# Delta-rule and retention gates in pairs of chunks, half of their rows as seven block products for eight

## The chip, the cores and the metric

The kernel runs on one core of a Trainium2 chip. The core has five engines that run side by side, each working through its own list of instructions in order: PE (matrix products), DVE (element-wise vector work), ACT (activations and copies), POOL (a small general engine) and SP (which here only issues transfers). Sixteen DMA engines move data between the chip's memory (HBM) and the core's own (SBUF, 128 partitions). Products are summed in PSUM, eight banks of 128x512 float32. The metric is the time of one execution on the device in microseconds.

## What is computed

One layer of a streaming encoder on 256 tokens, width 2048, all in float32. `h = rms_norm(x)`; one wide projection of h feeds two token mixers; their outputs are gated, added and projected; then cross-attention into 256 memory tokens and a squared-ReLU MLP. Around the change:

```python
proj = h @ w_in
(rq, rk, rv, rg, gqkv, ga, gb, gz, gate_a, gate_b) = jnp.split(proj, ...)
yr = retention_chunked(rope(rq), rope(rk) * RET_DK ** -0.5, rv)   # then normalised per head
yr = silu(rg) * yr
yg = gated_delta_chunked(gq, gk, gv, log_a, beta)  # per chunk of 64: triangular solve of (eye + m)
yg = silu(gz) * (yg * rsqrt(mean(yg * yg) + NORM_EPS) * gdn_norm_g)
merged = sigmoid(gate_a) * yr + sigmoid(gate_b) * yg
```

rg, gz, gate_a and gate_b are each 2048 columns wide: h (256x2048) times a 2048x2048 part of w_in.

## The kernel before

**Three products for one.** PE multiplies in a faster form of float32 with fewer bits. Each operand is therefore split into a rounded part (hi, copied by ACT) and what is left (lo, subtracted by DVE), and a product is three: hi hi, hi lo, lo hi. For weights, `fetch` (line 106) loads 1 MB into a buffer `raw` (three in turn) on SP's queue, and per half of it (128x1024) ACT writes `whi` (line 124) and DVE `wlo` (line 125), three buffers of each. h stands split in four tiles h1[0..3], each with four of the sixteen 128-row blocks of the inner dimension.

**Chunks.** `chunk` (line 156) makes 512 columns of a projection for all 256 tokens: four fetches of 1 MB (q = 0..3, a quarter of the inner dimension each), and for each 4 blocks x 2 token tiles x 3 products of 128x512, so 96 in all, summed in two banks (`stream_ps`, tags s0 and s1, two of each). `blocks` (line 226) makes 256 columns in turned form for the parts that need features on partitions.

**The mixer** is a loop over four groups j of heads (line 969), each 512 columns wide, with a fifth turn for what is left:

1. `gdn_stream(j)`: projections of q, k, v for the delta rule in two pairs of heads; short convolution; k and q products of a pair (lines 700, 702, "grams"); scaled and masked into `alt`; small diagonal blocks copied into `cmp_l` (line 728). `kq` holds a pair's k and q.
2. `gdn_blocks(j)`: the diagonal blocks go to HBM and come back turned round (`scr_l`, `lw`, lines 755 to 758), a triangular solve of 62 dependent operations on DVE (lines 766 and 768) fills `tw`, which goes out (`scr_t`, line 770) and comes back as `ct` (line 776).
3. `gate_delta_rule(j - 1)` (j > 0): the chunks gz and gate_b of the group before, their gating, then a transpose (`to_feature`).
4. `retention(j)`: two `blocks` projections into `qk`, one chunk of v into `vh` and `vl`, scores and outputs, normalisation.
5. `gdn_core(j)`: the rest of the delta rule, written as steps that `step()` lets run one at a time between the products of the following chunks.
6. `gate_retention(j)`: the chunks rg and gate_a of this group.

So in turn j, groups 1 to 3, the delta-rule gates of group j - 1 follow the projections of group j, and the solve of group j runs beside them; in the fifth turn the gates of group 3 stand alone.

**What sets the order.** A scheduler orders each engine's list when the program is built, by priorities and by data: fetches and roundings have a high priority, and a tile that is written waits until the last reader of what lay in its buffer is done. Tiles with the same tag and `bufs=1` share one buffer. All small PSUM results come from `bank()` (line 74), tag b, four banks in turn. On an engine, an instruction that waits holds up everything behind it.

In the MLP, the second product already uses seven block products for eight (`with_seven`, line 1202), on sums of tokens made by `token_sums`.

Of the kernel before, what the change touches and what calls it, by code (L numbers as in the profile page):

```python
# [54 lines left out]
def trunk(ctx: ExitStack, tc: tile.TileContext, x_f, mem_f, positions, lead_f, small_f, w_blocks, w_chunks, w_ga,  # L55
# [136 lines left out]
    def cols(w, c):  # L192
        return lambda q: w[c, q]
# [472 lines left out]
    def gdn_stream(grp):  # L666
# [3 lines left out]
        for pr in range(2):  # L670
# [17 lines left out]
                r4 = mx.tile([P, 4, NT, GD], F32, name="r4", tag="r4", bufs=1)  # L688
            grams = []
            ssk, ssq = (mx.tile([P, 2, NT], F32, name=nm, tag=nm, bufs=2) for nm in ("ssk", "ssq"))  # L690
            for b in range(2):
                kh = mx.tile([P, 2, S], F32R, name="kh", tag="kh", bufs=2)
                kl = mx.tile([P, 2, S], F32R, name="kl", tag="kl", bufs=2)
                act.activation(kh, kq[:, b], AF.Copy)
                vec.tensor_sub(kl, kq[:, b], kh.bitcast(F32))
                g0, g1 = bank(), bank()
                g0v = g0.rearrange("p (a n) -> p a n", a=2)
                g1v = g1[:, 0:256].rearrange("p (a n) -> p a n", a=2)
                for n, (l, r) in enumerate(((kh, kh), (kh, kl), (kl, kh))):
                    pe.matmul(g0v, l[:, 0, 0:P], r, start=n == 0, stop=n == 2)  # L700
                for n, (l, r) in enumerate(((kh, kh), (kh, kl), (kl, kh))):
                    pe.matmul(g1v, l[:, 0, P:S], r[:, :, P:S], start=n == 0, stop=n == 2)
# [165 lines left out]
    def retention(j, yr):  # L868
# [36 lines left out]
        for t in range(NT):  # L905
            ops = bank()
            for e in range(2):
                es = slice(e * 256, (e + 1) * 256)
                for m in range(t + 1):
                    ns = slice((t + m) * P, (t + m + 1) * P)  # L910
                    three(ops[:, es], [a[:, ns] for a in sts[e]], [a[:, m, es] for a in v], m == 0, m == t)
            mv = mx.tile([P, 2, 2], F32, name="mv", tag="mv", bufs=2)
            for e in range(2):
                bs = mx.tile([P, 6], F32, name="bs", tag="bs", bufs=2)
                vec.bn_stats(bs, ops[:, e * 256:(e + 1) * 256])
                vec.bn_aggr(mv[:, e, :], bs)
            ve = mx.tile([P, 2], F32, name="ve", tag="ve", bufs=2)
            vec.tensor_scalar(ve, mv[:, :, 1], 1e-5, None, op0=ALU.add)
            rg = mx.tile([P, 2], F32, name="rg", tag="rg", bufs=2)
            rsqrt(rg, ve)  # L920
            for e in range(2):
                es = slice(e * 256, (e + 1) * 256)
                vec.tensor_scalar(yr[:, t, es], ops[:, es], mv[:, e, 0:1], rg[:, e:e + 1],
                                  op0=ALU.subtract, op1=ALU.mult)
            vec.tensor_mul(yr[:, t, :], yr[:, t, :], gng)


    def gates():
        def gate_of(ps, f, scale):
            th = mx.tile([P, 512], F32, name="gth", tag="gth", bufs=1)  # L930
            act.activation(th, ps, f, scale=scale)
            return th

        def silu_gate(y):
            def evac(t, ps, c0, c1):
                th = gate_of(ps, AF.Silu, 1.0)
                vec.scalar_tensor_tensor(y[:, t, :], th, 0.5, y[:, t, :], op0=ALU.mult, op1=ALU.mult)
            return evac

        def sig_gate(y, other=None):  # L940
            def evac(t, ps, c0, c1):
                th = gate_of(ps, AF.Tanh, 0.5)
                vec.scalar_tensor_tensor(y[:, t, :], th, 1.0, y[:, t, :], op0=ALU.add, op1=ALU.mult)
                if other is not None:
                    vec.tensor_add(y[:, t, :], y[:, t, :], other[:, t, :])
            return evac

        def of_retention(j, yr):
            chunk(h1, cols(w_chunks, H_RG + j), silu_gate(yr))
            chunk(h1, cols(w_chunks, H_TA + j), sig_gate(yr))  # L950

        def of_delta_rule(j, yr, yg, quad, before=None):
            chunk(h1, cols(w_chunks, H_GZ + j), silu_gate(yg))
            chunk(h1, cols(w_chunks, H_TB + j), sig_gate(yg, yr), before=before, cuts=2 if before else 1)
            to_feature(lambda t, f: yg[:, t, f * P:(f + 1) * P], quad)

        return of_retention, of_delta_rule
# [10 lines left out]
    gate_retention, gate_delta_rule = gates()  # L968
    for j in range(5):
        if j < 4:  # L970
            heads, cmp_l, r4, qe4 = gdn_stream(j)
            solved = gdn_blocks(heads, cmp_l)
        if j:
# [510 lines left out]
```

## Time and profile before

| | |
|---|---|
| time, median of 3 runs (lowest to highest) | 2041.7 us (2041.68 to 2042.55) |
| profiled execution, its own time | 2043.06 us |
| its span | 2041.3 us |
| granted PE clock, mean | 0.998 |
| products on PE, in the trace | 10790 |
| HBM read | 389.74 MB |

A row of the timelines is start, length, engine, line, operation, what is written and read, shapes, count, and in brackets the idle time of the engine before it with what ended it. PE's length of a product is longer than its pitch, as products are pipelined: the pitch is the distance of starts. An instruction list's "idle before" is the time in which that engine stood still ahead of these instructions.

### The profile page before, as it was taken

To read this page: it belongs to the slowest core of one execution; us is meant where nothing else is said; L and a number is where in the kernel's file an instruction comes from. 1 tells how busy PE (TensorE), PEld (TensorE's weight loads), DVE (VectorE), ACT (ScalarE), POOL (GpSimd) and SP (SyncE) were. 2 spreads that over 40 slices of the span, in tenths; PEclk is the share of its full clock that TensorE was granted. 3 is DMA by queue.
4 is the path that set the end of the run, shared out by engine and by line. 5 is a ranking of instruction groups with operands and counts; after the bars stand their busy time and mean duration, and the time that the engine had idled before them with its cause. 6 is when DMAs were issued, how large, how long until landed. Compare 5 with 4: busy or idle time off the path is not lost.

```text
span 2041.3 us, 28479 instructions
## 1 busy us (share of the span) xinstructions
PE 2030.2 (99%) x10790; PEld 1751.3 (86%) x10790; DVE 1563.3 (77%) x2423; ACT 1203.0 (59%) x1981; POOL 39.9 (2%) x50
## 2 busy tenths in 40 slices
PE   9999999999999999999999999999999999999998
PEld 8888888988888888888888899888888888888886
DVE  5887788679668875788557666777887887888788
ACT  5655764575457554755446565566556656655665
POOL 0000000000000000000000000000000000000000
PEclk9999999999999999999999999999999999999999
DMA  8678556455555554555457554568636545554661
GB/s 326 210 267 289 185 182 199 163 186 189 185 178 181 191 185 165 189 191 194 145 206 251 195 184 155 186 207 276 218 125 233 217 168 209 204 205 168 235 238 62
DMA packets 79642, 405.24 MB, mean 199 GB/s; under 512 B 16512, under 2 KB 24592, under 8 KB 34832
## 3 DMA queue, kind: packets, MB, share of 16 engines
q1 hardware_dynamic: 79072, 402.74, 56.9%
q8 instruction: 84, 1.38, 0.3%
q10 hardware_dynamic: 432, 0.69, 0.1%
q14 instruction: 54, 0.44, 0.1%
HBM read 389.74 MB, written 11.55 MB: 197 GB/s over the span
## 4 chain that ended last, share of the span: by engine, by line
PE 96%; DVE 2%; DMA 1%; issue 0%; ACT 0%; SPq 0%; POOLq 0%; DVEq 0%; POOL 0%; ACTq 0%
PE s L213 51%; PE s L170 8%; PE s L171 8%; PE s L169 8%; PE s L1230 7%; PE b L1230 7%; PE s L402 1%; PE s L403 1%; PE s L404 1%; PE b L797 1%; PE b L141 1%; PE b L830 1%; PE b L140 1%; PE b L142 1%; PE b L700 0%
## 5 line engine op out<-in xcount | busy, mean ns | idle before, releaser
L213 PE MATMUL s<-q,whi 128*128 128x512 f32 x2824 | 971.7, 391 | 0.0
L125 DVE TENSOR_TENSOR wlo<-raw,whi 128x1024 fp32r<-128x1024 f32 x599 | 730.4, 1221 | 284.2 <-ACT whi L124 279.6
L124 ACT ACTIVATE whi<-raw 128x1024 fp32r<-128x1024 f32 x599 | 635.2, 1061 | 500.3 <-PE s L213 218.8
L213 PE MATMUL s<-q,wlo 128*128 128x256 f32 x2824 | 766.1, 281 | 0.2 <-DVE wlo L125 0.2
L213 PEld LDWEIGHTS s<-q,whi 128*128 128x128 f32 x2824 | 521.8, 188 | 101.0
L213 PEld LDWEIGHTS s<-q,wlo 128*128 128x128 f32 x2824 | 528.7, 188 | 13.4 <-DVE wlo L125 0.7
L170 PE MATMUL s<-wlo,q 128*128 128x512 f32 x704 | 277.2, 394 | 0.0
L171 PE MATMUL s<-whi,q 128*128 128x512 f32 x704 | 274.9, 391 | 0.0
L169 PE MATMUL s<-whi,q 128*128 128x512 f32 x704 | 254.4, 391 | 0.0
L169 PEld LDWEIGHTS s<-whi,q 128*128 128x128 f32 x704 | 132.1, 188 | 27.3
L171 PEld LDWEIGHTS s<-whi,q 128*128 128x128 f32 x704 | 132.3, 188 | 26.3
L170 PEld LDWEIGHTS s<-wlo,q 128*128 128x128 f32 x704 | 132.3, 188 | 26.2
L222 ACT ACTIVATE bo<-s 128x256 f32<-128x256 f32 x192 | 73.3, 382 | 110.0 <-PE s L213 109.9
L1230 PE MATMUL s<-whi,q 128*128 128x512 f32 x384 | 122.1, 389 | 0.0
L223 DVE TENSOR_TENSOR bo<-bo,s 128x256 f32<-128x256 f32 x192 | 79.6, 415 | 41.9 <-ACT bo L222 41.5
L1253 DVE TENSOR_TENSOR wlo<-rt,whi 128x1024 fp32r<-128x1024 f32 x55 | 67.3, 1224 | 35.9 <-ACT whi L1252 35.5
L213 PE MATMUL s<-q,whx 128*128 128x512 f32 x248 | 86.6, 390 | 0.0
L1230 PEld LDWEIGHTS s<-whi,q 128*128 128x128 f32 x384 | 72.1, 188 | 14.9
L1252 ACT ACTIVATE whi<-rt 128x1024 fp32r<-128x1024 f32 x55 | 58.2, 1059 | 41.8 <-PE s L1230 29.4
L1230 PE MATMUL s<-wlo,q 128*128 128x512 f32 x192 | 74.7, 389 | 0.0
L213 PE MATMUL s<-q,wlx 128*128 128x256 f32 x248 | 68.2, 280 | 0.0
L1230 PE MATMUL b<-whi,q 128*128 128x512 f32 x208 | 67.2, 389 | 0.0
(353 smaller groups left out, 2326.9 us busy)
## 6 DMA issues: line engine op xcount, KB each, us to landing
raw<-w_ff SPq DMA_DIRECT2D x96, 1024.0 KB
raw<-w_chunks SPq DMA_DIRECT2D x79, 1024.0 KB
raw<-w_blocks SPq DMA_DIRECT2D x64, 1024.0 KB
raw<-w_xk SPq DMA_DIRECT2D x16, 1024.0 KB
raw<-w_out SPq DMA_DIRECT2D x16, 1024.0 KB
raw<-w_xq SPq DMA_DIRECT2D x16, 1024.0 KB
raw<-w_xo SPq DMA_DIRECT2D x16, 1024.0 KB
rt<-w_ff SPq DMA_DIRECT2D x16, 1024.0 KB
```

What stands on the lines that cost most here:

```text
L124: latest["hi"] = act.activation(hi[:, cs], src[:, cs], AF.Copy).ins
L125: latest["lo"] = vec.tensor_sub(lo[:, cs], src[:, cs], hi[:, cs].bitcast(F32)).ins
L140: pe.matmul(o, lhs[0], rhs[0], start=first, stop=False)
L169: pe.matmul(o, xh, wh, start=first, stop=False)
L170: pe.matmul(o, xh, wl, start=False, stop=False)
L171: pe.matmul(o, xl, wh, start=False, stop=last)
L213: ins = pe.matmul(ps[b][:, :S] if part else ps[b], halves[h][part][:, i, b * P:(b + 1) * P], x[:, kk % 4, :], start=kk == 0 and not part, ...
L222: act.activation(o, ps[b][:, S:], AF.Copy)
L223: vec.tensor_add(o, o, ps[b][:, :S])
L1230: ins = pe.matmul(o, lhs[l], rhs[r], start=key not in opened, stop=last and j == 2, skip_group_check=True).ins
L1252: latest["hi"] = act.activation(hi, raw[:, c:c + 1024], AF.Copy).ins
L1253: latest["lo"] = vec.tensor_sub(lo, raw[:, c:c + 1024], hi.bitcast(F32)).ins
```

## The change

The two chunks of a gate stage are made together by a new function `two_chunks`, for the retention gates of groups 1 to 3 and the delta-rule gates of all four groups; the retention gates of group 0 stay as two chunks. Of the four quarters of the inner dimension, q = 2 and 3 are plain products for both chunks (`plain`, 24 products each). Quarters 0 and 1 form a 2x2 scheme: two halves of tokens (128 each), the two quarters, the two chunks. Instead of eight block products of 12 it makes seven (`product`), each of a sum of token blocks with a sum of weight blocks:

- The sums of tokens come once from `sums_of_tokens` on DVE in the projections of group 1 and stay in `s_in` (sh, sl).
- The sums of weight blocks are formed in x (1 MB in two half tiles xa, xb) and y (ya, yb). One block is loaded by SP (`load_parts`), and another is added to it either by DVE (`add_to`) or by a transfer from POOL's queue that adds into its destination (`add_parts`). In the delta-rule pairs all four additions are such transfers; in the retention pairs two are, and two are DVE's.
- x and y have no buffers of their own: xa shares the tag of `kq`, xb that of `lw`, ya that of `qk`, yb that of `tw`. u and d, which hold shared products that are added into the results at the end, share those of `vh` and `vl`; so do k's two parts in `gdn_stream`.
- The results are completed when they are read: `gate_of` adds u or d to the PSUM result on DVE before the activation.
- `bank()` now has two tags, b and c, with two banks each; while a pair runs, it holds the two of c, and everything else has the two of b.
- Retention's outputs are copied from PSUM by ACT before their normalisation, and the scratch for software-made transfer descriptors is set to 4096.

```diff
-    def bank():
-        return psp.tile([P, 512], F32, name="b", tag="b", bufs=4)
+    taken, kept_back = [0], []
+
+    def bank(tag=None):
+        if not tag:
+            taken[0] += not kept_back
+            tag = "b" if kept_back or taken[0] % 2 else "c"
+        return psp.tile([P, 512], F32, name="b", tag=tag, bufs=2)
...
+            act.activation(yr[:, t, :], ops, AF.Copy)
...
+    def two_chunks(chunks, evacs, before=None, moved=("x2", "x4")):
+        own = [stream_ps(), stream_ps()]
+        shared, p5 = bank("c"), bank("c")
+        kept_back.append(None)
+        x, y = ([mx.tile([P, 1024], F32, name=n, tag=tag, bufs=1) for n, tag in these]
+                for these in ((("xa", "kq"), ("xb", "lw")), (("ya", "qk"), ("yb", "tw"))))
...
+        def load_parts(to, n, q):
+            with tc.high_priority(offset=100000), tc.issue_after(fetched[-1]):
+                for h in range(2):
+                    fetched.append(nc.sync.dma_start(to[h], lines(n, q, h)).ins)
+
+        def add_parts(to, n, q):
+            with tc.high_priority(offset=100000):
+                for h in range(2):
+                    pool.dma_start(to[h], lines(n, q, h), accum_op=ALU.add)
...
+        def triple(o, lhs, rhs, key):
+            for l, r in ((0, 0), (0, 1), (1, 0)):
+                with tc.issue_after(ends[-1]) if ends else ExitStack():
+                    ins = pe.matmul(o, lhs[l], rhs[r], start=key not in opened, stop=False, skip_group_check=True).ins
...
+        plain(0, 2)
+        load_parts(x, 1, 0)
+        if "x1" in moved:
+            add_parts(x, 0, 0)
+        b11 = load(0, 0)
+        product(shared, part(0, 0), b11, "shared")
+        if "x1" not in moved:
+            add_to(x, b11)
+        with tc.high_priority(offset=50000):
+            u = kept_sum("vh", shared)
+        u1, u3 = u[:, 0], u[:, 1]
+        product(p5, summed(0), x, "p5")
+        add_parts(x, 1, 1)
+        plain(0, 3)
+        load_parts(y, 1, 0)
+        if "y" in moved:
+            add_parts(y, 1, 1)
+        b22 = load(1, 1)
+        product(own[1][0], summed(3), b22, (1, 0))
+        if "y" not in moved:
+            add_to(y, b22)
+        product(shared, summed(1), x, "shared")
+        add_parts(x, 0, 1)
...
+        plain(1, 2)
+        b21 = load(0, 1)
+        product(own[0][0], part(1, 0), b21, (0, 0))
+        finish(0, 0, u1)
+        product(shared, summed(2), y, "shared")
...
+        product(own[0][1], part(1, 1), x, (0, 1))
...
+        plain(1, 3)
...
+            if j in (1, 2, 3):
+                two_chunks((H_RG + j, H_TA + j), (silu_gate(yr), sig_gate(yr)))
+                return
...
+            if j in (0, 1, 2, 3):
+                two_chunks((H_GZ + j, H_TB + j), (silu_gate(yg), sig_gate(yg, yr)), before, ("x1", "x2", "x4", "y"))
```

How the change moves instructions, at the delta-rule gates of group 2, which stand in turn 3 with the solve of group 3. First DVE, at the beginning of that solve (pr and tw are the solve; wlo are roundings of weights). Before:

```order
L125 TENSOR_TENSOR wlo<-raw,whi 128x1024
L766 TENSOR_TENSOR pr<-lw,tw 32x31
L768 TENSOR_TENSOR tw<-tw,pr 32x31
L766 TENSOR_TENSOR pr<-lw,tw 32x60
L768 TENSOR_TENSOR tw<-tw,pr 32x30x2
L766 TENSOR_TENSOR pr<-lw,tw 32x87
L768 TENSOR_TENSOR tw<-tw,pr 32x29x3
L125 TENSOR_TENSOR wlo<-raw,whi 128x1024
L766 TENSOR_TENSOR pr<-lw,tw 32x112
L768 TENSOR_TENSOR tw<-tw,pr 32x28x4
L766 TENSOR_TENSOR pr<-lw,tw 32x135
L768 TENSOR_TENSOR tw<-tw,pr 32x27x5
```

Now, the end of it and what follows (after its first row and the rounding of xa, the solve's other 61 rows stand without any row between them):

```order
L773 TENSOR_TENSOR tw<-tw,pr 32x2x30
L771 TENSOR_TENSOR pr<-lw,tw 32x31
L773 TENSOR_TENSOR tw<-tw,pr 32x31
L787 COPY t_1857<-ct 32x4x32 x4
L783 STREAM_TRANSPOSE cu<-ct 128x256
L991 TENSOR_TENSOR wlo<-xb,whi 128x1024
L788 COPY u_1859<-cu 32x4x32 x4
L991 TENSOR_TENSOR wlo<-raw,whi 128x1024 x4
L991 TENSOR_TENSOR wlo<-xa,whi 128x1024
L991 TENSOR_TENSOR wlo<-xb,whi 128x1024
```

The roundings that stood between the solve's rows now stand behind it, the one of xb first. Next SP at the same place (scr_l, lw, scr_t and ct are the solve's transfers). Before:

```order
L112 DMA raw<-w_chunks 128x2048 x5
L755 DMA scr_l<-cmp_l 128x256
L112 DMA raw<-w_chunks 128x2048
L758 DMA lw<-scr_l 8x32x32 x4
L112 DMA raw<-w_chunks 128x2048 x2
L112 DMA raw<-w_blocks 128x2048 x4
L112 DMA raw<-w_chunks 128x2048 x4
L770 DMA scr_t<-tw 32x1024
```

And now:

```order
L966 DMA ya<-w_chunks 128x1024
L982 DMA raw<-w_chunks 128x2048 x2
L966 DMA xa<-w_chunks 128x1024
L760 DMA scr_l<-cmp_l 128x256
L763 DMA lw<-scr_l 8x32x32 x4
L966 DMA xb<-w_chunks 128x1024
L775 DMA scr_t<-tw 32x1024
L966 DMA yb<-w_chunks 128x1024
L781 DMA ct<-scr_t 32x8x32 x4
L982 DMA raw<-w_chunks 128x2048 x2
```

The loads of weights that stood between lw and scr_t are gone from there; in their place is the half-load of xb, and all later loads stand behind scr_t. Last PE, from the transposes that end the projections of the group. Before:

```order
L739 MATMUL b<-ident,vt 128x128 x2
L741 MATMUL b<-ident,kq 128x128 x2
L170 MATMUL s_8710<-wlo,q 128x512
L171 MATMUL s_8710<-whi,q 128x512
L170 MATMUL s_8711<-wlo,q 128x512
L171 MATMUL s_8711<-whi,q 128x512
```

And now (sh and sl are the sums of tokens, so the rows with sh belong to the product with x, of which the first two are shown):

```order
L746 MATMUL b<-ident,kq 128x128 x2
L998 MATMUL b<-whi,q 128x512
L998 MATMUL b<-wlo,q 128x512
L998 MATMUL b<-whi,q 128x512 x2
L998 MATMUL b<-wlo,q 128x512
L998 MATMUL b<-whi,q 128x512 x2
L998 MATMUL b<-wlo,q 128x512
L998 MATMUL b<-whi,q 128x512 x2
L998 MATMUL b<-wlo,q 128x512
L998 MATMUL b<-whi,q 128x512
L998 MATMUL b<-whi,sh 128x512
L998 MATMUL b<-wlo,sh 128x512
```

The plain quarter (0, 2) has moved ahead of these transposes, and behind them stand one block product and the product with x, with no other work of PE between them.

More of the change, by code (lines that the diff above doesn't have):

```diff
@@ L928, in gates, with gate_of @@
     def gates():
-        def gate_of(ps, f, scale):
+        def gate_of(ps, f, scale, more):
             th = mx.tile([P, 512], F32, name="gth", tag="gth", bufs=1)
+            if more is not None:
+                vec.tensor_add(th, ps, more)
+                ps = th
             act.activation(th, ps, f, scale=scale)
@@ L970, in trunk @@
         if j < 4:
+            if j == 1:
+                for i in range(4):
+                    turns.extend(4 * [lambda: None] + [lambda i=i: sums_of_tokens(i)])
             heads, cmp_l, r4, qe4 = gdn_stream(j)
```

101 lines of the change are left out of this document (90 added, 11 removed).

## The prediction

> **What bounds the kernel now.** I read the page's busy shares and its chain first, then the chain of waits in order of time, then busy time by stage, and last the timelines of one stage, engine by engine.
>
> ```profile
> span 2041.3 us, 28479 instructions
> PE 2030.2 (99%) x10790; PEld 1751.3 (86%) x10790; DVE 1563.3 (77%) x2423; ACT 1203.0 (59%) x1981; POOL 39.9 (2%) x50
> PE 96%; DVE 2%; DMA 1%; issue 0%; ACT 0%; SPq 0%; POOLq 0%; DVEq 0%; POOL 0%; ACTq 0%
> ```
>
> PE is busy all the time and the chain that ended last is 96% PE, so a product that disappears is worth its pitch, and any time in which PE has nothing to run is added to the end in full. The pitch is in the chain of waits, where 108 products of 128x512 run without a break in the tail (start, length, what):
>
> ```profile
> 1451.34 24.48 PE s L1230 x108
> ```
>
> 24.48 / 108 = 0.2267 us each. The next question is how full the other engines are where the change lands. The window view (length, then busy us by engine, the granted clock, the DMA share, GB/s) of three gate stages, each two chunks long: the delta-rule gates of group 2, the retention gates of group 3, and the last delta-rule gates:
>
> ```profile
> 868.00:915.00 47.00, 47.00 (x216) 39.04 (x215) 38.75 (x80) 27.38 (x57) 1.01 (x1) 1.00 0.57 186
> 965.00:1020.00 55.00, 55.00 (x290) 47.11 (x290) 33.19 (x58) 25.42 (x46) 3.91 (x4) 1.00 0.45 153
> 1020.00:1065.00 45.00, 45.00 (x209) 37.55 (x208) 26.05 (x25) 21.54 (x23) 0.00 (x0) 1.00 0.55 189
> ```
>
> DVE is 82% busy in the first. What fills it is the group's triangular solve, a chain of 62 dependent small operations (lines 766 and 768) that starts here and is woven between the weight roundings (line 125):
>
> ```profile
> L125 DVE TENSOR_TENSOR wlo<-raw,whi 128x1024 fp32r<-128x1024 f32 x19 | 23.1, 1214 | 1.5 <-ACT whi L124 1.5
> L768 DVE TENSOR_TENSOR tw<-tw,pr 32x31 f32<-32x31 f32 (+15 forms) x31 | 10.2, 328 | 0.6
> L766 DVE TENSOR_TENSOR pr<-lw,tw 32x31 f32<-32x31 f32 (+15 forms) x31 | 10.1, 327 | 1.8 <-DMA lw<-scr_l 1.3
> L943 DVE SCALAR_TENSOR_TENSOR yg<-gth,yg 128x512 f32<-128x512 f32 x2 | 1.4, 683 | 0.0
> ```
>
> (Groups of DVE between 888.9 and 938.4 us: count, busy us, mean ns, idle before.) Before, nobody waits for that chain until retention has ended: PE is 47.00 of 47.00 us busy across it.
>
> **What the change removes.** A pair of chunks is 2 x 96 products now. After, it is 4 x 24 plain ones and 7 x 12 block ones, 180. Twelve fewer in each of seven pairs: 84 x 0.2267 = 19.0 us. That is all it can gain.
>
> **What it adds: a wait for the solve, in three of the four delta pairs.** x and y, which hold the sums of weight blocks, have no room of their own: the second half of x lies in lw, the solve's input, the second half of y in tw, its result. The rows of the order on SP show the half-load of xb behind lw and ahead of scr_t, the store that follows the solve; on DVE the 62 operations stand with no weight rounding but xa's among them, and xb's rounding comes after the last of them; on PE the product with x follows the first eight transposes, one plain quarter and one block product. In groups 1 to 3 the solve is the one of the same loop turn, so x's second half cannot be loaded until it is done. Now the time of that, from group 3's turn. PE's last projection product and the first product after it:
>
> ```profile
> 867.23 0.28 PE L213 MATMUL s<-q,wlo 128*128 128x256 f32 x1
> 867.35 0.39 PE L700 MATMUL b<-kh 128*128 128x512 f32 x1
> 867.58 0.28 PE L702 MATMUL b<-kh 128*128 128x256 f32 x1
> 867.70 0.40 PE L169 MATMUL s<-whi,q 128*128 128x512 f32 x1
> ```
>
> Call 867.35 zero. The solve's input is ready when ACT has copied the last blocks, SP stores it and fetches it turned round, and the solve starts:
>
> ```profile
> 880.20 1.04 ACT L728 ACTIVATE cmp_l<-alt 32x64 f32<-32x64 f32 x4
> ...
> 881.26 0.33 SPq L755 DMA_DIRECT2D scr_l<-cmp_l  x1
> 882.94 1.89 SPq L758 DMA_DIRECT2D lw<-scr_l  x4
> ...
> 888.91 0.18 DVE L766 TENSOR_TENSOR pr<-lw,tw 32x31 f32<-32x31 f32 x1 [1.28 <-DMA lw<-scr_l]
> 889.12 0.20 DVE L768 TENSOR_TENSOR tw<-tw,pr 32x31 f32<-32x31 f32 x1
> 889.36 0.21 DVE L766 TENSOR_TENSOR pr<-lw,tw 32x60 f32<-32x60 f32 x1
> 889.61 0.21 DVE L768 TENSOR_TENSOR tw<-tw,pr 32x60 f32<-32x60 f32 x1
> 889.85 0.24 DVE L766 TENSOR_TENSOR pr<-lw,tw 32x87 f32<-32x87 f32 x1
> 890.12 0.24 DVE L768 TENSOR_TENSOR tw<-tw,pr 32x87 f32<-32x87 f32 x1
> 890.29 1.21 DVE L125 TENSOR_TENSOR wlo<-raw,whi 128x1024 fp32r<-128x1024 f32 x1
> 891.42 0.26 DVE L766 TENSOR_TENSOR pr<-lw,tw 32x112 f32<-32x112 f32 x1
> ```
>
> Step by step: input ready at +13.9 (881.24); store and fetch to the first operation 7.65, so +21.55; the solve alone 10.1 + 10.2 = 20.3 of operations, and gaps of 0.034 (888.91 to 890.12 is 1.21 for five that last 1.04) 61 times, 2.1, so 22.4; xa's rounding inside it 1.13 (890.29 to 891.42). The last read of lw is at about +45.1. Then come a half-load of 512 KB for xb and the adding transfer of another 512 KB into it, one after the other. The nearest rows for such a load:
>
> ```profile
> 273.69 0.33 SPq L755 DMA_DIRECT2D scr_l<-cmp_l  x1
> 275.39 1.92 SPq L758 DMA_DIRECT2D lw<-scr_l  x4
> ...
> 1067.91 0.42 SPq L1064 DMA_DIRECT2D kr<-kt_d  x1
> ...
> 1073.71 1.06 ACT L136 ACTIVATE kth<-kr 128x1024 fp32r<-128x1024 f32 x1 [2.72 <-DMA kr<-kt_d]
> ```
>
> 128 KB land in 1.7 us, and 512 KB behind other traffic in 5.8. I take 3.5 for the plain load, since SP has nothing else in flight by then. No row of this trace is an adding transfer. Its lower bound is the plain load, 3.5; its upper, as it reads both addends, twice the slowest such load, 11.6. I take 5, nearer the plain one, because the queue is empty here too. The Trainium skill (DMA: Bandwidth & Descriptors, Anatomy of one DMA — SWDGE (gpsimd) path) gives about 2.0 us plus the bytes over 436 GB/s, which would be 3.2 us here as an estimate and would take 5.4 us off the sum below over three pairs; no run here shows it yet.
>
> ACT and DVE then round the half, 1.06 and 1.13, and PE's second product of it needs both: 2.0 for the part that shows. PE restarts on it at 45.1 + 3.5 + 5 + 2.0 = +55.6. In the meantime PE has 24 products of plain(0,2), 12 of b11 and the 6 of x's first half, 42 x 0.2267 = 9.5; six pairs of gram products at 0.35 (867.35 to 867.70), 2.1; and eight transposes, 0.8:
>
> ```profile
> 880.91 0.38 PE L739 MATMUL b<-ident,vt 128*128 128x128 f32 x2
> ...
> 881.71 0.48 PE L170 MATMUL s<-wlo,q 128*128 128x512 f32 x1
> ```
>
> That is 12.4, so PE stands still for 55.6 - 12.4 = **43.2 us per pair**. Nothing else can run: the pair holds both accumulator sets, so retention's projections, next on PE, cannot start.
>
> After a stall PE does not come back at full pace. At the kernel's start the products are 0.43 apart until 10.32 and 0.23 apart after:
>
> ```profile
> 8.61 0.63 PE L403 MATMUL s<-wlo,q 128*128 128x512 f32 x1
> 9.04 0.63 PE L404 MATMUL s<-whi,q 128*128 128x512 f32 x1
> ...
> 10.32 0.83 PE L402 MATMUL s<-whi,q 128*128 128x512 f32 x2
> 10.99 0.62 PE L403 MATMUL s<-wlo,q 128*128 128x512 f32 x2
> 11.45 0.62 PE L402 MATMUL s<-whi,q 128*128 128x512 f32 x2
> ```
>
> The first product with weights is some 5.3 us before that change, so up to 2.6 us are lost each time; I take 2. The Trainium skill (TensorE: Matmul & The Clock Gate, Part 1) says that the array falls to half its clock after an idle window of about 3.4 us and needs about 3.4 us of work to come back. By that rule the loss is 1.7 instead of 2, 0.9 us less in the sum; the start-up rows agree in kind. And the roundings of the next quarter, held behind xb's on both ACT and DVE, need one more round of 1.1 to 3 us before PE is ahead again: 1.5. Together 46.7 per pair, 140.1 for three.
>
> **The rest.** DVE gets six more roundings a pair (22 for 16), and for each pair four adds and two subtractions of 128x512 (0.68 each). In the retention pairs four additions of 128x1024 come on top, since x1 and y stay on DVE there: 10 x 1.22 + 6 x 0.68 = 16.3 us on the 33.2 of the second window, 49.5 in 55 - 2.7 = 52.3. That is 95% full, with the steps of the delta rule's core threaded through it, each with fewer products between them than before and two PSUM buffers in turn instead of four. I expect these three pairs to give back what they save, 2.7 each (bounds 0, if PE stays fed, and 10, if every core step waits for a backlog of some four roundings once or twice). The last delta pair has no solve in its way; DVE goes to some 37 of 42 us, but 13 transfers of 1 MB in 40.8 us of products are 334 GB/s, and five of them add:
>
> ```profile
> DMA  8678556455555554555457554568636545554661
> GB/s 326 210 267 289 185 182 199 163 186 189 185 178 181 191 185 165 189 191 194 145 206 251 195 184 155 186 207 276 218 125 233 217 168 209 204 205 168 235 238 62
> ```
>
> The fullest slice had 326 GB/s at eight to nine tenths. I add 3 for it (0, as some lands ahead, to 12). The token sums (28 operations of at most 0.68, some 10 us of DVE in the projections of group 1), the copies out of PSUM and the narrower scratch for descriptors I cost at nothing, covered by PE's work on projections; if that cover is gone, 5 us at most. The MLP only changes the order of a few rows: 0.
>
> Sum against the profiled execution's own 2043.06 (span 2041.3): 2043.1 - 19.0 + 140.1 + 8.2 + 3 = 2175.4. The median of the runs shown is 1.4 lower, so **2174 us**, 6.5% slower.
>
> **The rivals.** *Faster: the solve is out of the way in time.* PE would lose nothing but small waits: 2041.7 - 19.0 + 8.2 + 3 = 2034. It decides where the stall per pair is under 19.0 / 3 = 6.3 us, that is where x's second half is rounded by +18.7. The store of the solve's input is only issued at +13.9 and landed at +21.55 above, before a single operation, so only a dependency that I read wrongly could do this. Chance 0.04. *Slow adding transfers.* At 11.6 each instead of 5, the three delta pairs lose 6.6 more each; in all seven the sum of x for the third product has some 8.2 us of PE work less 2 of rounding as cover, so 5.6 more, and the next some 2.7: 2174 + 20 + 58 = 2252. For it: two addends, software-made descriptors. Against: the DMA engines are half idle. Chance 0.08. *A short stall:* half the chain overlaps after all, as DVE is freed of the roundings that ran there before: 20 us a pair less, 2174 - 60 = 2114. Against it: each step needs the one ahead. Chance 0.05.
>
> **How the numbers follow.** The forecast has 0.83. Its own terms: start of the solve 2 us earlier or later, load 1.7 to 5.8, add 3.5 to 11.6, restart and catch-up 0 to 5.6, retention 0 to 10 a pair, last 0 to 12. All lower ends at once make 37.9 a pair and 2136; all upper ends 59.7 a pair and 2245, which will not all meet. With the short stall below and most of the upper side, the range is 2120 to 2225. About 0.2% (4 us) is what a measurement can tell from no change: faster by more 0.04, within 0.01, slower 0.95.
>
> **What would show it.** PE's idle groups by releaser should show three stalls of 35 to 50 us, at the block product after the first in delta pairs 0 to 2, released by DVE's rounding of xb; DVE's timeline 62 solve operations back to back in some 23 us; the page 84 products fewer (10706) and PE's share near 93%; the load of xb right after the last row with lw, and 3 to 12 us for the adding one. No idle stretch above 10 us in the retention pairs. The forecast is wrong if PE runs through the solve, or if the lost time lies in all seven pairs alike.

## The result, and the profile after

| | time, median (lowest to highest) | against before, 95% interval |
|---|---|---|
| before | 2042.1 us (2041.68 to 2042.97) | |
| after | 2188.5 us (2187.44 to 2189.77) | 1.0717 (1.0704 to 1.073) |

The kernel is 146.4 us slower. The forecast was 2174 us in a range of 2120 to 2225. The page of after:

```profile
span 2188.1 us, 28742 instructions
...
PE 2034.5 (93%) x10706; PEld 1743.3 (80%) x10706; DVE 1664.0 (76%) x2547; ACT 1263.5 (58%) x2056; POOL 80.4 (4%) x94
...
PE   9999999919998299974998999999999999999998
...
PEclk9999999969999599986998999999999999999999
```

The 84 products are gone (10706 for 10790), yet PE is busy for 4 us longer than before and idle for 154 us. The slices, 54.7 us each, show where: three holes, at the ninth slice, the fourteenth and the nineteenth, with the granted clock down to 0.5 to 0.6 around each. The table of waits on PE (engine, tile and line that wait, what released them, us in total, times, longest) says that one kind of wait makes nearly all of it:

```profile
PE b L998 <- ACT whi L990: 130.3, 8, 33.2
PE b L998 <- DVE wlo L991: 7.1, 12, 1.1
PE b L744 <- DVE alt L725: 3.2, 3, 1.1
```

Line 998 is the product inside a pair, line 990 ACT's rounding of a half. Here is the third hole, turn 3, in the timelines of PE, ACT, SP, DVE and POOL, put in order of time. 955.73 is the zero of the prediction's sum, the first gram product:

```profile
955.73 0.39 PE L705 MATMUL b<-kh 128*128 128x512 f32 x1
...
968.83 1.03 ACT L733 ACTIVATE cmp_l<-alt 32x64 f32<-32x64 f32 x4
969.89 0.33 SPq L760 DMA_DIRECT2D scr_l<-cmp_l  x1
971.64 2.24 SPq L763 DMA_DIRECT2D lw<-scr_l  x4
977.16 0.79 PE L998 MATMUL b<-whi,sh 128*128 128x512 f32 x1 [8.15 <-ACT whi L990]
977.67 0.18 DVE L771 TENSOR_TENSOR pr<-lw,tw 32x31 f32<-32x31 f32 x1 [5.32 <-DMA lw<-scr_l]
977.80 1.23 DVE L991 TENSOR_TENSOR wlo<-xa,whi 128x1024 fp32r<-128x1024 f32 x1
...
1000.89 0.18 DVE L771 TENSOR_TENSOR pr<-lw,tw 32x31 f32<-32x31 f32 x1
1001.10 0.36 SPq L966 DMA_DIRECT2D xb<-w_chunks  x1
1005.68 0.86 POOL L971 DMA_DIRECT2D xb<-w_chunks  x1 [25.51 <-DMA scr_t<-tw]
1013.65 1.06 ACT L990 ACTIVATE whi<-xb 128x1024 fp32r<-128x1024 f32 x1 [36.54 <-DMA xb<-w_chunks]
1014.76 0.80 PE L998 MATMUL b<-whi,sh 128*128 128x512 f32 x1 [33.17 <-ACT whi L990]
1016.16 0.79 PE L998 MATMUL b<-wlo,sh 128*128 128x512 f32 x1 [0.61 <-DVE wlo L991]
```

To be read as one chain: the solve's input is stored at +14.2, the solve starts at +21.9, its last read of lw ends at +45.3, the load of xb leaves 30 ns later, the adding transfer follows it 4.6 us after and takes 8.0 us, and PE has the hi part of the half at +59.0 and both parts at +60.4. PE stands idle in this pair for 44.4 us in two pieces: 8.2 us for the first half of x and 33.2 us for the second, and small change.

How the stages grew, read from the starts of PE's rows: a delta pair with a solve (last product of the stream to the first of the unbroken run of retention projections) took 46.8 us each before and takes 93.2, 94.2 and 94.6 now, 141.6 more in all. The stretch from there to the next stream went from 101.2 and 101.1 to 98.6 and 98.7, so the first two retention pairs *gain* 2.5 each. The third with the last delta pair went from 144.7 to 153.7, so with 2.5 gained there too the last delta pair loses 11.5.

### The profile page after: what moved, and what is told of

It reads as the page before. It is cut to its first block, busy times and chain, and to the rows that moved or that the text cites. A ratio compares the mean times of both kernels' runs of the same rounds, so it can differ in the third digit from the quotient of the medians.

```text
span 2188.1 us, 28742 instructions
## 1 busy us (share of the span) xinstructions
PE 2034.5 (93%) x10706; PEld 1743.3 (80%) x10706; DVE 1664.0 (76%) x2547; ACT 1263.5 (58%) x2056; POOL 80.4 (4%) x94
## 4 chain that ended last, share of the span: by engine, by line
PE 84%; DVE 8%; DMA 4%; issue 2%; ACT 1%; SPq 0%; POOL 0%; POOLq 0%; DVEq 0%; ACTq 0%
PE s L218 48%; PE s L998 7%; PE s L1396 7%; PE b L1396 6%; PE s L175 3%; PE s L176 3%; PE s L174 3%; PE b L998 2%; DVE tw L773 1%; DVE pr L771 1%; DVE wlo L991 1%; DMA ct<-scr_t 1%; DMA xb<-w_chunks 1%; PE s L407 1%; PE s L408 1%
## 5 line engine op out<-in xcount | busy, mean ns | idle before, releaser
L130 DVE TENSOR_TENSOR wlo<-raw,whi 128x1024 fp32r<-128x1024 f32 x467 | 570.2, 1222 | 205.5 <-ACT whi L129 201.5
L129 ACT ACTIVATE whi<-raw 128x1024 fp32r<-128x1024 f32 x467 | 495.2, 1060 | 330.0 <-PE s L218 195.4
L998 PE MATMUL s<-whi,q 128*128 128x512 f32 x560 | 181.1, 396 | 0.0
L998 PE MATMUL b<-whi,sh 128*128 128x512 f32 x84 | 38.5, 458 | 130.3 <-ACT whi L990 130.3
L991 DVE TENSOR_TENSOR wlo<-raw,whi 128x1024 fp32r<-128x1024 f32 x98 | 119.2, 1223 | 34.3 <-ACT whi L990 33.6
L990 ACT ACTIVATE whi<-raw 128x1024 fp32r<-128x1024 f32 x98 | 103.1, 1057 | 55.0 <-PE s L998 31.6
L998 PEld LDWEIGHTS b<-whi,sh 128*128 128x128 f32 x84 | 17.7, 211 | 138.6 <-ACT whi L990 134.9
L998 PEld LDWEIGHTS s<-whi,q 128*128 128x128 f32 x560 | 107.3, 192 | 22.6
L998 PE MATMUL s<-wlo,q 128*128 128x512 f32 x280 | 111.6, 398 | 0.0
L1419 DVE TENSOR_TENSOR wlo<-rt,whi 128x1024 fp32r<-128x1024 f32 x62 | 75.5, 1224 | 39.4 <-ACT whi L1418 39.0
L175 PE MATMUL s<-wlo,q 128*128 128x512 f32 x256 | 101.0, 395 | 0.0
L176 PE MATMUL s<-whi,q 128*128 128x512 f32 x256 | 99.8, 390 | 0.0
L1396 PE MATMUL s<-whi,q 128*128 128x512 f32 x288 | 93.0, 389 | 0.0
L1418 ACT ACTIVATE whi<-rt 128x1024 fp32r<-128x1024 f32 x62 | 65.7, 1060 | 44.4 <-PE s L1396 25.6
L174 PE MATMUL s<-whi,q 128*128 128x512 f32 x256 | 90.2, 390 | 0.0
L990 ACT ACTIVATE whi<-xb 128x1024 fp32r<-128x1024 f32 x21 | 22.2, 1058 | 117.7 <-DMA xb<-w_chunks 111.3
```

The source lines that it names most:

```text
L129: latest["hi"] = act.activation(hi[:, cs], src[:, cs], AF.Copy).ins
L130: latest["lo"] = vec.tensor_sub(lo[:, cs], src[:, cs], hi[:, cs].bitcast(F32)).ins
L174: pe.matmul(o, xh, wh, start=first, stop=False)
L175: pe.matmul(o, xh, wl, start=False, stop=False)
L176: pe.matmul(o, xl, wh, start=False, stop=last)
L990: latest["hi"] = act.activation(hi, src, AF.Copy).ins
```

## The experiments

The theory: the loss is the wait for the solve, and it exists because x's second half lies in lw and y's second half in tw. The rivals: adding transfers are slow, or DVE (the vector engine) has too much to do. Four kernels make a square of the two edits that can be made apart, the sharing of room and the way in which delta pairs form their sums; the rest look into what is left.

### Retention pairs alone (e1)

```diff
-            if j in (0, 1, 2, 3):
+            if j in ():
                 two_chunks((H_GZ + j, H_TB + j), ...
```

> All four delta pairs go back to two separate chunks each; the three retention pairs stay in twos, with their scratch in lw and tw, the token sums, the PSUM copies and the narrower descriptor scratch. Theory (the loss is the wait for the solve in delta pairs 0 to 2): all of the loss is gone, and the three retention pairs keep the 2.5 us each that the trace of after shows, so 2042.1 - 7.5 = 2034.6 (2033 to 2038). Rival (the work common to all pairs, copies, token sums, narrower scratch, costs something): between 2042 and 2060. Rival (the prediction's own term, that retention pairs give back what they save): 2042.

Measured: 2036.7 us, 0.9974 of before (0.9965 to 0.9983). The 146 us are gone, and the kernel is 5.4 us faster than before. All that the change adds in common, copies out of PSUM, token sums, narrower scratch, costs less than the retention pairs gain. PE's waits of this kernel fall to nothing:

```profile
PE b L998 <- DVE wlo L991: 0.5, 3, 0.2
```

### The square: other room (e2), other sums (e3), both (e5)

The edit to the room, for delta pairs 0 to 2, is that of e2; that of e3 is the list of sums that are made by adding transfers:

```diff
-                for these in ((("xa", "kq"), ("xb", "lw")), (("ya", "qk"), ("yb", "tw"))))
+                for these in ((("xa", "kq"), ("xb", "g_a" if room is not None else "lw")),
+                              (("ya", "qk"),) if room is not None else (("ya", "qk"), ("yb", "tw"))))
+        if room is not None:
+            y.append(room.rearrange("p a s -> p (a s)"))   # room: the pair's own mg tile
```

```diff
-  ... before, ("x1", "x2", "x4", "y"))
+  ... before)                                   # ("x2", "x4"), as in retention pairs
```

> The sharing alone is undone: in delta pairs 0 to 2 the second half of x lies in the core's room g_a, free at that time, and the second half of y in the pair's own mg tile, which is written only at the pair's end. All seven pairs stay in twos, all adding transfers, all 62 solve operations and the same work on DVE stay. Theory: the three stalls of 44 us are gone. If these pairs then do as well as the retention pairs (2.5 us better than before each) the time is 2042.1 - 7.5 - 7.5 + 11.4 = 2038.5; if they do as badly as the last delta pair (11.4 worse each) 2042.1 - 7.5 + 4 x 11.4 = 2080; so 2036 to 2080. Rival (DVE's load or the adding transfers make the stall, and the sharing is only where it shows): 2150 to 2190.

> Delta pairs take two of their four sums with adds on DVE, as retention pairs do, in place of adding transfers; the sharing stays. Theory: the three stalls stay, shorter by what the adding transfer of x's second half takes (8.0 us from issue to landing in the trace of after) less one addition of 1.2 us, so some 6 us each, and the last pair's 6 us wait for its second adding transfer may go: 2188.5 - 18 - 0 to 8 = 2162 to 2171. Rival (adding transfers are what costs): under 2100.

> Both edits together: no sharing in delta pairs 0 to 2, and two of four sums on DVE in all four delta pairs. Theory: no stall from the solve; against the run with the other room alone it tells what the adding transfers cost once the sharing is gone. If transfers bunch as in the last delta pair of after, this run is 5 to 40 us faster than that one, at 2030 to 2045; if DVE, which has the solve and 22 roundings in a pair, is what lacks, it is slower than that one by 3 x 2.4 (two additions of 1.2) up to 20 us.

| | sums by adding transfers | two of four on DVE | difference |
|---|---|---|---|
| second halves in lw and tw | after: 2188.5 | e3: 2165.5 | 23.0 |
| second halves elsewhere | e2: 2099.0 | e5: 2075.4 | 23.6 |
| difference | 89.5 | 90.1 | |

The ratios to before are 1.0281 (1.0264 to 1.0299) for e2, 1.0605 (1.0589 to 1.0621) for e3, 1.0165 (1.0149 to 1.018) for e5. The two effects add, within 0.6 us: 90 us are the sharing, 23 the adding transfers. The rival that blames the transfers alone is out (e3 would have been under 2100). In e3 the gain was not quite where it was expected: the three pairs gave 2.0, 4.5 and 5.0 us (6 each expected), the stretch with the last pair 9.7. And e2 is 19 us above the upper end that the theory gave it, e5 30 above its own, so the wait for the solve covered up other waits, which show when it goes. In e2, turn 3 (SP, POOL, ACT and PE in order of time):

```profile
909.50 0.38 PE L746 MATMUL b<-ident,kq 128*128 128x128 f32 x2
909.91 0.33 SPq L969 DMA_DIRECT2D xa<-w_chunks  x1
...
917.90 0.90 POOL L974 DMA_DIRECT2D xa<-w_chunks  x1 [9.31 <-DMA xa<-w_chunks]
...
924.20 1.06 ACT L993 ACTIVATE whi<-xa 128x1024 fp32r<-128x1024 f32 x1 [7.72 <-DMA xa<-w_chunks]
925.31 0.80 PE L1001 MATMUL b<-whi,sh 128*128 128x512 f32 x1 [12.12 <-ACT whi L993]
```

The first half of x is late too. Its room is kq, which holds the group's keys and queries until the last transposes of the queries (909.50, already among the pair's products); the load can leave at 909.91 only, takes 8.0 us beside other loads, and the adding transfer 6.3 more.

### The solve left out (e4)

```diff
-        for j in range(31):
+        for j in range(0):
             n = 31 - j
             ... 62 operations on lw and tw
```

> The kernel after, with the 62 operations of the solve left out in all four turns (tw stays the identity); stores, fetches, sharing and adding transfers stay. Theory (the solve's own length is in the wait of three pairs): 3 x 22.4 = 67 us less than after: 2121, with PE idle for some 21 us per pair instead of 44, since store, fetch, load and adding transfer stay in the chain. Rival (the wait is for transfers, and the solve only lies ahead of them): less than 20 us gained, over 2165.

Measured, in two runs: 2125.9 us, 62.6 less than after, for 67 expected. With the small waits, PE is idle for 21.9 us in the pair of turn 3, as expected. The two waits of about 10 us in it are the two chains of load and adding transfer, for x's first half and for its second (PE, turn 3):

```profile
938.23 0.80 PE L998 MATMUL b<-whi,sh 128*128 128x512 f32 x1 [9.77 <-ACT whi L990]
...
951.85 0.79 PE L998 MATMUL b<-whi,sh 128*128 128x512 f32 x1 [9.86 <-ACT whi L990]
```

### What is left once the sharing is gone (e6, e7, e8)

e5 loses 37 us against the same kernel with delta pairs 0 to 2 as two chunks each (e10, below): 12.5 a pair. Three candidates: x's first half late in kq, DVE's load with the solve, or the order of the products.

```diff
 e6 (on e2), e7 (on e5): first halves change places in delta pairs 0 to 2
-  (("xa", "kq"), ("xb", "g_a")), (("ya", "qk"),)
+  (("xa", "qk"), ("xb", "g_a")), (("ya", "kq"),)
 e8 (on e5): the solve left out, as in e4
```

> As the run with the other room (e2), and a second sharing undone: in delta pairs 0 to 2 the first half of x moves from kq, which holds the group's keys and queries until its last transposes inside the pair, to qk, free since the retention pair before; the first half of y, needed later, goes to kq in its place. In e2 that load left at 909.91 and the half was summed at 924.2, with PE idle 12.1 us for it. Theory (what e2 still lost is x late for a second reason, 12 to 13.5 us of idle and some 4 us at half pace a pair): 2099 less 3 x (14 to 18) = 2045 to 2057. Rival (adding transfers that bunch up, wherever x lies): 2085 to 2100.

> The same two changes of room, with two of the four sums of delta pairs on DVE. Theory: the 2.3 us waits for x that the run e5 still showed go, and the half pace behind them, some 6 us a pair: 2075.4 - 18 = 2057, or below where the transposes no longer wait for alt behind DVE's additions (2.2 us a pair): 2040 to 2060. Rival (DVE's 50 us of work in 44 us of products bounds the pair): 2070 to 2080, no better than e5.

> As e5 (other room for the second halves, two of four sums on DVE), with the 62 operations of the solve left out in all turns. Nobody in the delta pair waits for the solve any more in e5, so what this run gains is what the solve costs as 20 us of work in DVE's queue. Theory (with half the products to each rounding, DVE is what delta pairs 0 to 2 run against, and the solve is in its way): 2075.4 less 3 x 5 to 10 = 2045 to 2060. Rival (what is left in e5 is x's load behind the transposes and the half pace after it, whatever DVE does): 2070 to 2077.

Measured: e6 2099.4 (1.0271, 1.0254 to 1.0289), e7 2078.2 (1.0177, 1.0161 to 1.0194), e8 2078.5 (1.018, 1.0166 to 1.0194). All three theories missed: none of them is better than the kernel on which it stands. e6 landed where its rival had it. The longest waits on PE of e6, whose x is early:

```profile
PE b L1001 <- ACT junk L293: 17.5, 3, 7.5
PE s L1001 <- DVE wlo L994: 16.4, 13, 7.6
```

and of e8, which has no solve:

```profile
PE b L1001 <- ACT whi L993: 10.0, 3, 3.8
PE b L1001 <- DVE wlo L994: 7.7, 9, 1.5
PE b L744 <- DVE alt L725: 6.9, 3, 2.5
PE s L1001 <- DVE wlo L994: 6.3, 4, 3.3
```

With x early, the first product with x waits at the same place for something else: ACT's last sum of squares over the transposed queries (line 293). That reader by the trace releases it; that what it releases is the PSUM bank which the product takes is read from the code, where both come out of tag c with two banks, and was not tried apart. In e7 the transposes wait longer than in e5, too: 13.4 us in three waits for alt (6.6 in e5), as both additions that form x now stand ahead of alt in DVE's list.

The longest waits of the second kind, for DVE's roundings, are not a want of DVE's time: DVE itself stands still, at an instruction whose transfer has not landed, with the rounding that PE needs behind it in its list. DVE in turn 3 of e6, and in turn 1 of e8:

```profile
926.77 0.18 DVE L771 TENSOR_TENSOR pr<-lw,tw 32x31 f32<-32x31 f32 x1 [10.62 <-DMA lw<-scr_l]
...
927.87 1.21 DVE L994 TENSOR_TENSOR wlo<-raw,whi 128x1024 fp32r<-128x1024 f32 x1
```

```profile
463.44 0.45 DVE L787 COPY t<-ct 32x128 f32<-32x128 f32 x2 [2.49 <-DMA ct<-scr_t]
...
465.35 1.23 DVE L994 TENSOR_TENSOR wlo<-raw,whi 128x1024 fp32r<-128x1024 f32 x1
```

In e6 it is the solve's first operation. The fetch of its input is issued at 917.31, just after two adding transfers (ya at 916.44, xb at 916.99), and lands 9.5 us later, where it took 6.0 in after; so a part of the rival's reason, transfers that bunch up, may hold here and was not tried apart. In e8, without the solve, it is the copy of ct, the solve's stored result on its way back. With the solve gone, x is also late in kq, as in e5. As these three runs read, each cause is covered by the next, so that one alone, taken away, gains nothing.

### Plain quarters first (e9, e11, e12)

```diff
         plain(0, 2)
+        plain(0, 3)
         load_parts(x, 1, 0)
         b11 = load(0, 0)
         product(shared, part(0, 0), b11, "shared")
         product(p5, summed(0), x, "p5")
         add_parts(x, 1, 1)
-        plain(0, 3)
+        plain(1, 2)
         ... b22, then x's second product
-        plain(1, 2)
         ... b21, y
-        product(own[0][1], part(1, 1), x, (0, 1))
         plain(1, 3)
+        product(own[0][1], part(1, 1), x, (0, 1))
```

> As e7 (both halves of x and y in room that is free early, two of four sums on DVE), and the order of the pair changed: two plain quarters stand ahead of the first block product and one ahead of b22, and the last product with x comes after the last plain quarter. A plain quarter gives PE 24 products for two roundings, a block product 12. Theory (roundings, on ACT behind the copies for the solve and on DVE beside it, come too late for block products in the first 20 us of the pair): the waits of 2 to 4 us and the half pace behind them go, some 10 us a pair: 2078 - 30 = 2048 (2038 to 2062). Rival (a bound by DVE's total work, which an order doesn't change): 2070 to 2080.

> As e7, with the order of e9 in delta pairs 0 to 2 alone; the retention pairs and the last delta pair keep the order of after, and the gates of both chunks are applied in the order of after for every row (in e9 and e11 the second gate, with the retention part added, came ahead of the first for half of the rows). Theory (the first block products of a pair with a solve come too early for their roundings): 20.6 us below e7 as in e9, and 2.0 to 3.9 more, since e11 showed the new order 3.9 us worse in the other four pairs: 2054 (2049 to 2059). Rival (e9's gain came from the four other pairs or from the order of the gates): 2070 to 2080.

Measured: e9 2057.6 (1.0074, 1.006 to 1.0088), 20.6 us below e7; e12 2069.0 (1.0124, 1.0107 to 1.0141), only 9.2 below e7, outside both forecasts. In e9 and e11 the second token tile's rows have the second gate, with the retention part added, ahead of the first gate, which changes the result and not the number of operations. The stretches on PE from the end of the stream to the end of the next retention projections are 85.1, 78.9 and 81.0 us in e7, 74.2, 73.2 and 72.6 in e9, and 73.7, 72.4 and 72.3 in e12 (70.2, 69.7 and 69.7 before). So in e12, too, the order takes 26.6 us out of the pairs themselves, about what the theory had. Most of what e12 lacks is lost in the stretch *after*: from the end of these projections to the next stream, 82.7 and 80.1 us in e12 against 76.3 and 76.3 in e7 and 76.7 and 76.0 in e9. Of the waits on PE of e12, one kind is nearly absent in e9:

```profile
PE b L802 <- DMA ct<-scr_t: 7.7, 3, 4.2
```

Line 802 is the first step of the delta rule's core, in the retention pair. Its chain of waits in order of time, in turn 3, begins at the solve's last operation:

```profile
985.70 0.19 DVE tw L773
...
986.11 3.77 DMA scr_t<-tw
...
992.23 8.67 DMA ct<-scr_t
...
1001.03 1.05 PE b L802 x8
```

The solve ends at 985.9, 26.6 us after the projections' end and 3.6 after the retention pair's first product; its result, stored and fetched again beside the pair's loads, is used 15.1 us further on. In turn 1 this wait is 4.2 us, and a stretch at half pace follows it. In e7 the solve of turn 3 ends 14.6 us after the projections, before the change 1.1. So what the better order wins, a late solve gives back in part: when the weight roundings go first, the 62 operations go later. In e9 the solve is as late as in e12 (26.6 us), but the retention pair has the new order as well, and the wait is there once, for 1.1 us; why it is so much shorter was not taken apart. How much of the rest is DVE's total and how much the order was not told apart; no run has the new order and no solve.

### The last delta pair (e10, e11)

```diff
-            if j in (0, 1, 2, 3):
+            if j in (3,):
                 two_chunks(..., before)      # two of four sums on DVE; e11: with the order of e9
```

> The three retention pairs and the last delta pair in twos, with two of its four sums on DVE; delta pairs 0 to 2 as before. In the run e3 the stretch with the third retention pair and the last delta pair took 118.6 us against 119.3 in e1, where it is not in twos: 2036.7 - 0.7 = 2036. If the second adding transfers bunch up as they did in after: 2041 to 2046.

> As e10, with the order of e9 in these four pairs. Theory (x's first sum gets 24 more products of cover): no wait for x in the last delta pair, 1 to 3 us under e10: 2032 to 2036. Rival (the order takes cover from x's third product, or delays the first products after the pair): no better than e10, or slower by 1 to 4 us.

Measured: e10 2038.1 (0.9981, 0.9972 to 0.999); e11 2041.9 (0.9999, 0.999 to 1.0008). The rival held for e11: without a solve in the way, the new order gains nothing and is 3.9 us slower than e10. In e10 the last pair costs 1.4 us against e1 (2036.7), which the two intervals do not tell from nothing, and its longest wait on PE is 0.9 us. With adding transfers alone, in after, the same pair waited for x's third sum (POOL, PE and ACT of after in order of time):

```profile
1156.01 0.88 POOL L971 DMA_DIRECT2D ya<-w_chunks  x1 [8.85 <-PE b L998]
1157.13 0.86 POOL L971 DMA_DIRECT2D yb<-w_chunks  x1 [0.23 <-issue]
1157.66 1.20 POOL L971 DMA_DIRECT2D xa<-w_chunks  x1
1158.50 1.25 POOL L971 DMA_DIRECT2D xb<-w_chunks  x1
...
1173.33 1.06 ACT L990 ACTIVATE whi<-xa 128x1024 fp32r<-128x1024 f32 x1 [9.51 <-DMA xa<-w_chunks]
1174.44 0.80 PE L998 MATMUL b<-whi,sh 128*128 128x512 f32 x1 [6.19 <-ACT whi L990]
...
1177.33 1.06 ACT L990 ACTIVATE whi<-xb 128x1024 fp32r<-128x1024 f32 x1 [2.94 <-DMA xb<-w_chunks]
```

Four adding transfers of 512 KB are issued within 2.5 us, and the two of x, last in the queue, are used 15.7 and 18.8 us after their issue.

### The ladder

Each rung is one edit, from the best kernel up to after:

| kernel | median | step | what the step is |
|---|---|---|---|
| before | 2042.1 | | |
| e1 | 2036.7 | -5.4 | retention pairs in twos |
| e10 | 2038.1 | +1.4 | last delta pair in twos |
| e5 | 2075.4 | +37.3 | delta pairs 0 to 2 in twos, other room |
| e3 | 2165.5 | +90.1 | second halves of x and y in lw and tw |
| after | 2188.5 | +23.0 | all sums of delta pairs by adding transfers |

The lowest median is that of e1, the change confined to the retention pairs; e10 is not told apart from it.

## Why the prediction was right, and where it was not

The forecast's place, cause and sign held. The terms of its sum, beside what the traces show:

| term | forecast | measured |
|---|---|---|
| 84 products fewer | -19.0 | -19.0 at the pitch of before |
| three delta pairs, loss beside the products | 140.1 | 149.8 (141.6 + 3 x 2.72) |
| retention pairs give back | 8.2 | 0.7 (2.5 of 2.72 kept each) |
| last delta pair | 3 | 14.2 (11.5 + 2.72) |
| rest (all up to group 1's stream -0.5, all after the mixer +1.4) | 0 | 0.9 |
| sum over before | 132.3 | 146.6 |

**The solve in the way.** Input ready, forecast +13.9, came at +14.1; the solve's start, +21.55, at +21.9; the last read of lw, +45.1, at +45.3. That 62 dependent operations run without a gap once nothing else may run was the strongest step, and e4 confirms the price: 62.6 us for three solves, 20.9 each, against 22.4.

**Load and adding transfer.** The load took 4.6 us for 3.5, the adding transfer 8.0 for 5, so PE had both parts of the half at +60.4 instead of +55.6. The bound of 11.6 was not reached here; the value was chosen too near the plain load, on the ground of an empty queue, and the queue was not empty: the load of yb and the four of ct left at the same time. The Trainium skill (DMA: Bandwidth & Descriptors, Anatomy of one DMA — SWDGE (gpsimd) path) gives 3.2 us for 512 KB as an estimate. The measurement disagrees: in after the summary of the tile xb has its 18 adding transfers, 512 KB each, at

```profile
DMA to landing us min/median/max: 5.4/7.6/18.7
```

**PE's cover** was 16.0 us, not 12.4, as the first half of x was itself 8.2 us late and what followed it ran at half pace; so the idle time came out at 44.4 against 43.2, two misses that nearly cancel. The prediction did not see that first wait at all: it took the first half of x as early, though it lies in kq. Under the sharing it cost nothing more, since the longer wait followed; e2 shows that it would have been the next bound. So the stall came in two pieces, and the long one is 32.3 to 33.2 us where the signs named 35 to 50; what ends it is ACT's rounding of xb, and DVE's, which the signs named, comes 0.6 us of idle time later.

**Half pace and catching up.** 3.5 us were forecast, and 5.5 are left of a pair's 49.9 after 44.4 of idle. The size was off; that the half clock is in it is seen (0.5 to 0.6 in the slices), how the rest divides is not.

**Retention pairs.** Wrong by 2.5 each, in reasoning too. The forecast had DVE 95% full there and made a loss of it. The window of the third retention pair of after (length, then busy us of PE, PEld, DVE, ACT and POOL, the granted clock, DMA share, GB/s):

```profile
1097.00:1152.00 55.00, 54.84 (x289) 46.60 (x289) 47.42 (x73) 34.72 (x59) 9.79 (x10) 1.00 0.74 208
```

DVE has 47.4 us of work in 55, close to the 49.5 that were reckoned, and PE misses 0.16. A vector engine that is busy for 86% of a stretch made PE wait for next to nothing here.

**Last delta pair.** Mis-sized: 3 for 14.2, beyond its bound of 12. The argument, that the DMA engines had room on average, missed that the transfers come in a bunch, in which one took 18.7 us, far beyond the bound of 11.6. e3 and e10 show it: with two sums on DVE the bunch and its wait are gone. (Four of the pair's 13 transfers add, not five as in the working, whose upper ends come to 2244, not 2245. Neither moves the forecast.)

**The rivals.** *Faster* decided at a stall under 6.3 us a pair; e2 to e12 show that even with the sharing undone no version of seven pairs came below 2057. *Slow adding transfers* named the right suspect for a part: 23 us, where it had 78. *A short stall* would have needed the chain to overlap; it did not.

## What to carry to other kernels

Room that is shared by tag is a dependency in time: before a buffer is given a second use, look up when its first use *ends* in the trace, and what must still happen to the new contents before the first consumer. Here that turned a solve which nobody waited for into the longest chain of the kernel. When one wait is taken out and the time moves less than the wait was long, the next late input was already standing behind it; edits should then be made as a square or a ladder, so that each has its own number. And a transformation that halves the matrix work for each prepared operand pays only where the operands are ready in time: the retention pairs kept 2.5 of 2.7 us each in the trace of after, and e1, with them alone, is 5.4 us faster than before; delta pairs 0 to 2 lost in every version, also without their solve (e8). On an engine that works in order, look for idle time as well as for busy time: an instruction that waits for a transfer holds up every rounding behind it.

## What the runs showed of the hardware

**A short pause can cost the clock, and later than it happened.** In e9, PE paused 1.86 us, went on at full pace for 1.6 us, and then ran six products at half pace, 0.43 apart (PE's timeline):

```profile
895.23 0.50 PE L1001 MATMUL b<-whi,sh 128*128 128x512 f32 x1 [1.86 <-ACT junk L293]
...
896.50 0.53 PE L1001 MATMUL b<-whi,sl 128*128 128x512 f32 x1
896.82 0.63 PE L1001 MATMUL b<-whi,sh 128*128 128x512 f32 x1
897.25 0.63 PE L1001 MATMUL b<-wlo,sh 128*128 128x512 f32 x1
```

The clock records of e9 show when: in the mixer the clock falls at 548.44, 674.73, 770.31 and 896.60, each time for 3.41 us, and these times lie 37, 28 and 37 steps of 3.413 us apart. The step that holds the pause and the one behind it, by windows of e9 (PE is busy for 1.55 us of the first; the granted clock is the third number from the end):

```profile
893.19:896.60 3.41, 1.55 (x7) 1.15 (x7) 2.85 (x4) 3.41 (x8) 1.02 (x2) 1.00 0.86 251
896.60:900.01 3.41, 3.41 (x10) 2.66 (x9) 2.01 (x2) 1.46 (x3) 0.74 (x1) 0.50 0.97 223
```

In e12 a pause of the same 1.86 us at the same place of turn 3 was followed by no such stretch. There a step ends at 904.11, within the pause, so that 0.4 us of it fall into one step and 1.5 into the next, and PE is busy for 3.02 us of the first and 1.94 of the second:

```profile
904.11:907.52 3.41, 1.94 (x8) 1.61 (x9) 3.41 (x4) 3.09 (x8) 1.59 (x2) 1.00 0.94 270
907.52:910.93 3.41, 3.41 (x16) 2.77 (x15) 1.81 (x4) 1.89 (x2) 0.17 (x1) 1.00 1.02 192
```

The Trainium skill (TensorE: Matmul & The Clock Gate, Part 1) has the clock fall after an idle window of about 3.4 us that runs free of the kernel. The steps agree with a free-running window; a pause of 1.86 us is shorter than that window, so here less than a whole idle window was enough. How little busy time a step may have is not settled: the fall at 770.31 in e9 came after a step with 2.27 us of it. In e5 the granted clock is at half in six stretches of the mixer, 30.7 us in all, so that some 15 us are lost (an estimate, half of it) beside an idle time of 25 us there: in that kernel short waits cost over half as much again as they lasted.

**Adding transfers** of 512 KB took 5.4 us at the least in after; the median is 5.9 for the tile xa and 7.6 for xb, and 18.7 was reached when four were issued together.
